# A hybrid decoder block on one core: the first pass's head outputs projected in seven products, with factor sums, gate sums and root rows moved

## The chip, the core and the metric

The kernel runs on one core of a Trainium2 chip. A core has five engines that run side by side, each with its own in-order stream of instructions: TensorE (PE), which multiplies matrices into the PSUM memory, VectorE (DVE), ScalarE (ACT), GpSimd (POOL) and SyncE (SP), which here issues the data transfers (DMAs). They meet through semaphores. The metric is the time of one execution on the device in microseconds (us), lower is better, as the median of three runs.

## The reference

A block over 2048 tokens of width D = 1024, in float32:

```
ada = silu(c) @ w_ada + b_ada;  shift, scale, gate = split(ada, 3)
h   = rms_norm(x, g_pre) * (1 + scale) + shift
pv, pg, hq, hf, hi, hg, mg_pool, mg_hgrn = split(h @ w_in)
branch_a = (pool(pv) * pool_scale * silu(pg)) @ w_pool_o     # 512 wide
o        = hgrn2(silu(hq), 1 - f, hi, log f)                 # 8 heads of 128; V is hi
branch_b = (rms_norm(o, hgrn_norm_g) * silu(hg)) @ w_hgrn_o  # 1024 x 1024
merged   = sigmoid(mg_pool) * branch_a + sigmoid(mg_hgrn) * branch_b
x + gate * rms_norm(merged @ w_out, g_post)
```

The change touches four places: V (`hi`), the gate row, `branch_b`'s projection by `w_hgrn_o`, and the preparation of `w_out`'s factors.

## The kernel before

The tokens go in two passes (p = 0 and 1) of 1024, each of two halves (t) of 512. Each float32 operand of a large product is split into a rounded part and the rest (`split`, L174: a copy on ACT, a subtraction on DVE), and a product is made of three matmuls: high by high, high by low, low by high (`three`, L352). A tile is 128 partitions by 512 columns (256 KB).

**Seven products.** A product of two 2x2 block matrices can be had from seven block products in place of eight, if sums of the blocks are multiplied. The kernel's names for the seven are B11, B21, T1, T2, T3, B22, T4. `quad` (L607) does this per head for the input projections, with T1 to T4 of h formed by `h_mix` (L594) and the weights' sums formed as they are loaded (`quad_items`, L211). `rows7` (L927) does it for a whole 1024 x 1024 projection: seven products of four row blocks by four factors by three matmuls, each of 128x512.

**The stages of a pass** are:
- V: `v_job` (L886), direct, in the first pass, in two halves of two column groups; `rows7` in the second;
- the heads, 8 of them, each with three `quad`s and the recurrence `hgrn` (L658) spread between them in steps (`tick`);
- the pool projection `a_job` (L1038), 8 jobs;
- the head outputs' projection: in the first pass `b_job` (L1048), eight jobs with two banks of 24 matmuls each, on head outputs split whole (`two_split`, L1016); in the second `b_fast` (L1096), on `rows7`. Its moving operands are sums of head outputs, formed by `g_half` (L1093) and `forms` (L1066), and split for the next product while one runs (`next_parts`, L1079);
- the output projection `y_fast` (L1138), on `rows7`, with the sums of merged columns formed by `forms("m", ...)` at the end of `b_fast`, or in `b_job`.

**Weights and their order.** `items` lists the weight tiles in the order of use. `take` (L338) hands out one and prepares some ahead (LOOK = 4) by `prep`: `plain_item` (L200) loads a tile raw and splits it, `whole_item` (L1243) does so with a prefetch two items earlier, and `again` (L195) reloads a tile that was split before and stored in DRAM, 512 KB at once. Raw tiles lie in a ring of seven (`wrp`), most other tiles in a pool of 76 (`utile`, L93).

**Factors.** The sums of weight blocks for `rows7` are formed once, ahead, by `row_factors` (L262): load four blocks, add and subtract, split some, and queue the result in `due` for storing. `htick` (L1425) does one step of it in 4 of 9 ticks of the heads. The first pass's heads form those of `w_out` ("y7") and of V ("v7", only the sums, which the second pass then splits), the second pass's heads those of `w_hgrn_o` ("b7", all seven stored split).

**The gate row.** `gate_sum` (L439) loads 8 tiles of `w_ada`, multiplies each by a column of silu(c) and adds up on DVE; `gate_out` (L453) sums over the partitions by a matmul with ones and goes through DRAM (`ggd`), from where `gg_in` (L1131) reads it before each output projection. Both halves of it lie within the first pass's `b_job`s, as do the two root rows (`r_row`, L533): matmuls that spread the inverse norms of the next pass's tokens over a tile.

**What sets the order.** The program text gives priorities. The framework that builds the kernel orders each engine's instructions by its own model of costs and buffers, so an engine's order in the trace isn't always the text's. `after` (L99) holds an instruction behind another; `gated` (L112) holds a load behind the last store. Loads and nearly all stores are on SP's queue, which is in order: a store that waits for DVE holds the loads behind it.

Of the kernel before, what the change touches and what calls it, by code (L numbers as in the profile page):

```python
# [8 lines left out]
F32 = mybir.dt.float32  # L9
# [62 lines left out]
def tile_block(ctx: ExitStack, tc: tile.TileContext, x, c, w_ada, b_ada, g_pre, g_post, w_in,  # L72
               pool_w, pool_scale, lb_logits, hgrn_norm_g, w_pool_o, w_hgrn_o, w_out,
               ident_d, mask_d, icnt_d, w_pv_t, x_t, w_quad, w_po, w_ho, out):
# [102 lines left out]
    def raw_load(name, srcs):  # L177
        raw = wrp.tile([P, T], F32, tag="wr", name=f"wr{name}")
        SP.dma_start(raw if srcs[1] is None else raw.rearrange("p (k n) -> p k n", n=srcs[1]), srcs[0])
        return raw  # L180
# [19 lines left out]
    def plain_item(key, src, n, keep_it):  # L200

        def make():
            name = f"{len(ready)}"
            if key in scr:
                return [again(key, name)]
            w = item_split(name, early.pop(key) if key in early else raw_load(name, (src, n)))
            keep(key, w, keep_it)
            return [w]
        items.append((1, make, None))
# [47 lines left out]
    def factor_step(steps):  # L257
        while due:
            store("due", *due.pop(0))
        once(steps)  # L260

    def row_factors(key, src, e, whole=(), skip=()):  # L262

        steps = []
        for i in range(4):
# [7 lines left out]
            def put(f, nm, i=i, r=r):  # L273
                if f in whole:
                    scr[key, f, i] = dram(f"scr_{key}_{f}_{i}", [P, T])
                    due.append((scr[key, f, i], r[nm]))
                    return
                w = [utile(f"rf{key}{f}{i}{z}", F32R) for z in range(2)]
                split(r[nm], w[0], w[1], e)
# [3 lines left out]

            def sums(r=r, i=i):
                r["s1"] = utile(f"rs{key}{i}")
                tt(r["s1"], r["21"], r["22"], op=ADD, e=e)

            def sub(o, a, b, r=r):
                tt(r[o], r[a], r[b], op=SUB, e=e)

            nop = lambda: None
            def both(f, g):
                return lambda: (f(), g())

            if whole:
                steps += [ld, nop, both(sums, lambda put=put: put(2, "s1")),
                          lambda sub=sub: sub("21", "11", "21"),
                          both(lambda sub=sub: sub("11", "s1", "11"), lambda put=put: (put(4, "21"), put(3, "11"))),
                          both(lambda sub=sub: sub("12", "12", "11"), lambda put=put: put(5, "12"))]
                continue  # L300
            todo = [(None, ld), (None, nop),
                    (0, lambda put=put: put(0, "11")),
                    (None, sums),
                    (1, lambda put=put: put(1, "12")),
                    (2, lambda put=put: put(2, "s1")),
                    (None, lambda sub=sub: sub("21", "11", "21")),
                    (None, lambda sub=sub: sub("11", "s1", "11")),
                    (3, lambda put=put: put(3, "11")),
                    (4, lambda put=put: put(4, "21")),
                    (None, lambda sub=sub: sub("12", "12", "11")),  # L310
                    (5, lambda put=put: put(5, "12")),
                    (6, lambda put=put: put(6, "22"))]
            steps += [g for f, g in todo if f not in skip]
# [125 lines left out]
    def gate_sum(n):  # L439
        acc = utile(f"gacc{n}")  # L440
        for kk in range(KT):
            wa = utile(f"wg{n}_{kk}")
            gated(wa, w_ada[kk * P:(kk + 1) * P, 2 * D + n * T:2 * D + (n + 1) * T])
            if kk == 0:
                V.tensor_scalar(acc, wa, cact[:, 0:1], None, op0=MUL)
            else:
                V.scalar_tensor_tensor(acc, wa, cact[:, kk:kk + 1], acc, op0=MUL, op1=ADD)
# [3 lines left out]
        return n, acc, bg, gp  # L451

    def gate_out(n, acc, bg, gp):  # L453
        ones = utile(f"ones{n}")[:, 0:P]
        G.memset(ones, 1.0)
        pg = px.tile([P, T], F32, tag="px", name=f"pgate{n}")
        PE.matmul(pg, lhsT=ones, rhs=acc, start=True, stop=True)
        V.tensor_tensor(bg, pg, bg, op=ADD)
        V.tensor_tensor(bg, gp, bg, op=MUL)
        store("gg", ggd[n], bg)  # L460
# [72 lines left out]
    def r_row(p, t, cx):  # L533

        pr = px.tile([P, T], F32, tag="px", name=f"pr{p}_{t}")
        dg = utile(f"dg{p}_{t}")
        for tk in range(NT):
# [3 lines left out]
            mm(pr[:, sl], one128, dg[:, sl], True, True)  # L541
# [452 lines left out]
    def two_out(nm, p, i, t, src, cx, stay):  # L994

        if stay and nm == "G" and p == NPASS - 1:
# [8 lines left out]
    def two_in(nm, p, i, cx):  # L1005
        for t in range(2):
            if nm == "G" and p == NPASS - 1:
# [13 lines left out]
    def sig_in(p, j, w, cx):  # L1021
# [4 lines left out]
        if nw < (1 if p == NPASS - 1 else 2):  # L1026
            cx["sm"][nj, nw] = sig_load(p, nj, nw, cx)
# [19 lines left out]

    def b_job(p, j, cx):  # L1048
        ps = [bank(f"psB{p}_{j}_{t}") for t in range(2)]
        sm = sig_in(p, j, 1, cx)  # L1050
        for half in range(2):
            w = take()
            for t in range(2):
                three(ps[t], w, [cx["gG"][4 * half + i, t] for i in range(4)], half == 0, half == 1)
        for t in range(2):
            a, b = cx["a"].pop((j, t)), sm[t]
# [515 lines left out]
```

## Time and profile before

| | us |
|---|---|
| median of 3 runs | 1751.21 |
| lowest and highest | 1750.67, 1752.98 |
| the profiled execution | 1752.19 |
| its span, first to last instruction | 1750.4 |
| ACT busy | 839.9 |
| POOL busy | 90.3 |
| TensorE's mean granted clock | 0.999 of full speed |

The stages in the profile of before: V of the first pass to about 124 us, the first pass's heads to about 685, the pool projection to 738.6, the head outputs' projection to 828.6, the output projection to 905; then the second pass. Of each slice of a fortieth of the span the page gives the busy share in tenths, and how many GB/s the DMAs moved:

```profile
DVE  4668897888988898666687265556566655676566
...
GB/s 313 266 182 312 300 279 274 285 295 267 289 300 294 277 247 279 186 203 91 231 326 182 267 252 233 249 228 214 257 240 226 230 192 206 167 252 200 250 186 265
```

The page lists groups of instructions by line, engine and operation, with the tiles that are written and read (buffer numbers left out), the count, the busy time and the mean duration of one, and the idle time of the engine ahead of them with its cause. A matmul's duration overlaps that of its neighbours, so what one costs is the distance from start to start. The chain of work follows the last instruction back to what released each step.

### The profile page before, as it was taken

The numbers are of one execution on the slowest core, as the hardware profiler recorded it, in microseconds if no ns is written. First come the engines' busy times: TensorE is split into PE (matmuls) and PEld (weight loads), VectorE is DVE, ScalarE is ACT, GpSimd is POOL, SyncE is SP. The second block draws the span as 40 slices with busy tenths as digits, with TensorE's granted clock in tenths as the row PEclk, the third lists the DMA queues.
The fourth block names the chain that finished last, engine by engine and source line by source line (L and its number), as shares of the span: only waits on it lengthen the run. The fifth ranks groups of instructions, "written<-read, shape, count | busy, mean of one in ns | idle before, by whom it ended". The sixth has DMA issues, their size and how long they took to land.

```text
span 1750.4 us, 31763 instructions
## 1 busy us (share of the span) xinstructions
PE 1725.4 (99%) x11853; PEld 1410.7 (81%) x11853; DVE 1208.6 (69%) x2516; ACT 839.9 (48%) x1953; POOL 90.3 (5%) x152
## 2 busy tenths in 40 slices
PE   7999999999999999999999999999999999999998
PEld 4788888888888887888888888888788788888886
DVE  4668897888988898666687265556566655676566
ACT  4746657566565565411655335344354352433243
POOL 1100000000010010000020000000000000000002
PEclk9999999999999999999999999999999999999999
DMA  9758877787888767562695877766776766575757
GB/s 313 266 182 312 300 279 274 285 295 267 289 300 294 277 247 279 186 203 91 231 326 182 267 252 233 249 228 214 257 240 226 230 192 206 167 252 200 250 186 265
DMA packets 193588, 428.47 MB, mean 245 GB/s; under 512 B 19565, under 2 KB 44826, under 8 KB 193434
## 3 DMA queue, kind: packets, MB, share of 16 engines
q1 hardware_dynamic: 184218, 409.66, 68.6%
q10 hardware_dynamic: 9216, 16.78, 2.5%
q8 instruction: 93, 1.52, 0.4%
q14 instruction: 61, 0.50, 0.1%
HBM read 264.36 MB, written 162.00 MB: 244 GB/s over the span
## 4 chain that ended last, share of the span: by engine, by line
PE 89%; DMA 5%; DVE 3%; ACT 1%; issue 1%; SPq 0%; POOL 0%; DVEq 0%; POOLq 0%; ACTq 0%
PE pafq L350 10%; PE pam L350 9%; PE pagp L350 9%; PE pem L350 5%; PE psB L350 5%; PE psA L350 5%; PE pefq L350 5%; PE pegp L350 5%; PE psa L350 4%; PE psV L350 3%; PE ray L350 3%; PE po L350 3%; PE pbfq L350 2%; PE pbgp L350 2%; PE pbm L350 2%; PE raB L350 2%
## 5 line engine op out<-in xcount | busy, mean ns | idle before, releaser
L175 ACT CAST whl<-wr 128x512 fp32r<-128x512 f32 x176 | 109.2, 621 | 99.6 <-PE psB L350 30.1
L175 DVE TENSOR_TENSOR whl<-wr,whl 128x512 fp32r<-128x512 f32 x176 | 120.3, 687 | 53.1 <-ACT whl L175 47.7
L350 PE MATMUL pam<-hT,whl 128*128 128x512 f32 x384 | 129.1, 397 | 0.4 <-ACT c12m L616 0.3
L350 PE MATMUL pagp<-hT,whl 128*128 128x512 f32 x384 | 128.2, 395 | 0.1
L350 PE MATMUL pafq<-hT,whl 128*128 128x512 f32 x384 | 126.2, 389 | 0.8 <-ACT c12fq L616 0.8
L714 DVE COPY_PREDICATED PT<-mask,psa 128x256 f32<-128x256 uint8 x160 | 86.4, 549 | 46.3 <-PE psa L350 46.3
L350 PEld LDWEIGHTS pagp<-hT,whl 128*128 128x128 f32 x384 | 72.1, 188 | 16.0 <-issue 0.5
L350 PEld LDWEIGHTS pafq<-hT,whl 128*128 128x128 f32 x384 | 72.1, 188 | 15.9 <-ACT c12fq L616 0.9
L350 PEld LDWEIGHTS pam<-hT,whl 128*128 128x128 f32 x384 | 72.1, 188 | 15.5 <-ACT c12m L616 0.7
L350 PE MATMUL psA<-Ph,whl 128*128 128x512 f32 x256 | 82.4, 395 | 0.1
L350 PE MATMUL psV<-whl,hB 128*128 128x512 f32 x256 | 79.6, 394 | 1.2 <-ACT hB L1324 1.1
L480 DVE TENSOR_TENSOR K<-K,TT 128x256 f32<-128x256 f32 x192 | 80.2, 424 | 0.1
L350 PE MATMUL psB<-Gh,whl 128*128 128x512 f32 x256 | 79.8, 392 | 0.0
L350 PE MATMUL pam<-lT,whl 128*128 128x512 f32 x192 | 74.9, 390 | 0.0
L350 PE MATMUL pagp<-lT,whl 128*128 128x512 f32 x192 | 74.9, 390 | 0.0
L350 PE MATMUL pafq<-lT,whl 128*128 128x512 f32 x192 | 74.7, 389 | 0.0
L175 ACT CAST whl<-wri 128x512 fp32r<-128x512 f32 x52 | 32.3, 622 | 83.1 <-PE raB L350 27.3
L350 PEld LDWEIGHTS psa<-X,K 128*32 128x32 f32 x2816 | 50.1, 110 | 26.1 <-issue 19.9
L350 PE MATMUL psa<-X,K 128*32 128x48 f32 (+2 forms) x2816 | 60.7, 208 | 0.0
L350 PEld LDWEIGHTS psV<-whl,hB 128*128 128x128 f32 x256 | 47.4, 188 | 13.9 <-ACT hB L1324 1.4
L825 POOL TENSOR_SCALAR ss<-ss 128x4 f32<-128x4 f32 x32 | 10.0, 312 | 901.5 <-ACT junk L824 901.3
L350 PEld LDWEIGHTS psA<-Ph,whl 128*128 128x128 f32 x256 | 48.0, 188 | 10.4 <-ACT Ph L175 0.5
(556 smaller groups left out, 4728.3 us busy)
## 6 DMA issues: line engine op xcount, KB each, us to landing
wr<-in_w_quad_dram SPq DMA_DIRECT2D x88, 256.0 KB, 4.0
whl<-scr_y SPq DMA_DIRECT2D x36, 512.0 KB, 4.3
sm<-Sd SPq DMA_DIRECT2D x64, 256.0 KB, 4.8
scr_b<-rfb SPq DMA_DIRECT2D x56, 256.0 KB, 3.0
whl<-scr_b SPq DMA_DIRECT2D x28, 512.0 KB, 4.1
scr_y<-rfy SPq DMA_DIRECT2D x40, 256.0 KB, 2.1
x<-in_x_dram SPq DMA_DIRECT2D x32, 256.0 KB, 4.3
wa<-in_w_ada_dram SPq DMA_DIRECT2D x32, 256.0 KB, 6.2
```

The lines of the kernel that those rows point to most:

```text
L175: return A.copy(hi, src32), (e or V).tensor_tensor(lo, src32, hi.bitcast(F32), op=SUB)
L350: return PE.matmul(o, lhsT=l, rhs=r, start=start, stop=stop, skip_group_check=True)
L480: return (e or V).tensor_tensor(o, a, b, op=op)
L714: V.copy_predicated(dst.rearrange("p (c q) a b -> p c q a b", c=NT), m, src.rearrange("p c (a b) -> p c a b", b=b).unsqueeze(2) .broadcast ...
L825: G.tensor_scalar(ss, ss, 1.0 / P, EPS, op0=MUL, op1=ADD)
```

## The change

- **Seven products in the first pass.** `b_job`, `two_split`'s use for head outputs and the host's rearranged copy of `w_hgrn_o` go; both passes use `g_half`, `forms` and `b_fast`. 
- **Factors.** Those of `w_hgrn_o` are formed in the first pass's heads, beside those of `w_out`; the second pass's heads form none. Of their seven, B11, B21 and B22 are no longer stored split: both passes load them raw and split them (`FORMED["b7"]`). The steps of `row_factors` are grouped anew, 68 in all as before.
- **V's factor sums** are formed in the first pass's V stage, from the raw tiles that were loaded there: these are kept (`vraw`; all but the first four lie in the pool of 76, and those of the second column group are loaded two items ahead), and `v_sums` adds them up at four places and queues four stores for each. The loads of V's weights in the heads go.
- **The gate** is loaded in eight steps and added in eight within `b_fast` (`gate_steps`). Its ones-matmul (`gate_sum`) and the rest (`gate_out`) lie in the first pass's output projection, which uses the tiles directly; DRAM is only for the second pass.
- **The root rows** lie in `b_fast`'s first two steps, in a bank of the ring of four.
- **Sums.** `b_fast` forms the merged columns' sums later: the first two sets at (B22, 2) and (T4, 0), the last two in the first two steps of `y_fast`. The scaling of the next pass's rows has written-out places, (T1, 1) to (T3, 0), in place of one for each step.

```diff
+    vraw = {}
+    def v_sums(i):
+        b11, b12, b21, b22 = (vraw.pop(z) for z in ((0, 2 * i), (0, 2 * i + 1), (1, 2 * i), (1, 2 * i + 1)))
+        V.tensor_tensor(b22, b21, b22, op=ADD)
+        V.tensor_tensor(b21, b11, b21, op=SUB)
+        V.tensor_tensor(b11, b22, b11, op=SUB)
+        V.tensor_tensor(b12, b12, b11, op=SUB)
+        for f, r in ((2, b22), (4, b21), (3, b11), (5, b12)):
+            scr["v7", f, i] = dram(f"scr_v7_{f}_{i}", [P, T])
+            due.append((scr["v7", f, i], r))
...
+    def gate_steps():
+        def ld(n, q):
+            gpart[n, q] = []
+            for kk in (2 * q, 2 * q + 1):
+                wa = utile(f"wg{n}_{kk}")
+                gated(wa, w_ada[kk * P:(kk + 1) * P, 2 * D + n * T:2 * D + (n + 1) * T])
+                gpart[n, q].append((kk, wa))
+        def add(n, q):
+            for kk, wa in gpart.pop((n, q)):
+                if kk == 0:
+                    gsum[n] = utile(f"gacc{n}")
+                    V.tensor_scalar(gsum[n], wa, cact[:, 0:1], None, op0=MUL)
+                else:
+                    V.scalar_tensor_tensor(gsum[n], wa, cact[:, kk:kk + 1], gsum[n], op0=MUL, op1=ADD)
...
-    FORMED = {"v7": (w_in[:, O_I:O_I + D], (0, 1, 6), (2, 3, 4, 5)), "y7": (w_out, (0, 1), ()), "b7": (w_hgrn_o, (), ())}
+    FORMED = {"v7": (w_in[:, O_I:O_I + D], (0, 1, 6), (2, 3, 4, 5)), "y7": (w_out, (0, 1), ()), "b7": (w_hgrn_o, (0, 1, 6), ())}
...
+            flush_due()
             v_job(p, t, grp, q, cx)
             if t == 0:
-                for _ in range(3 if p == 0 else 1):
+                for _ in range(3):
                     once(late)
-            elif q != 2:
+                if q > 1:
+                    v_sums(q - 2)
+            elif (grp, q) in ((0, 2), (1, 1)):
+                v_sums(2 + grp)
+            else:
                 once(mixes)
...
-        for key in (("y7", "v7"), ("b7",))[p]:
+        for key in (("b7", "y7"), ())[p]:
...
+        def b_step(nm, i):
+            if nm == "B11" and i < 2:
+                once(rows_r)
+            if nm in ("B21", "T1", "T2"):
+                once(g_loads)
+            if nm in ("T1", "T2"):
+                for _ in range(1 + i % 2):
+                    once(g_adds)
+        last_forms = b_fast(p, cx, [lambda: forms("g", 3, cx["g32"])], b_step)
```

More of the change, by code (lines that the diff above doesn't have):

```diff
@@ L273, in put @@
             def put(f, nm, i=i, r=r):
[L274 to L277, printed above, removed]
                 w = [utile(f"rf{key}{f}{i}{z}", F32R) for z in range(2)]
-                split(r[nm], w[0], w[1], e)
+                split(r[nm], w[0], w[1])
                 scr[key, f, i] = dram(f"scr_{key}_{f}_{i}", [P, 2 * T])
@@ L282, in put, with sub @@
                     due.append((scr[key, f, i][:, z * T:(z + 1) * T], w[z].bitcast(F32)))
+            def sub(o, a, b, r=r):
+                tt(r[o], r[a], r[b], op=SUB)
             def sums(r=r, i=i):
                 r["s1"] = utile(f"rs{key}{i}")
[L286 to L313, printed above, removed]
+                tt(r["s1"], r["21"], r["22"], op=ADD)
+            steps += [ld, lambda: None, sums,
+                      lambda put=put, sub=sub: (put(2, "s1"), sub("21", "11", "21")),
+                      lambda sub=sub: sub("11", "s1", "11"),
+                      lambda put=put: put(3, "11"),
+                      lambda put=put, sub=sub: (put(4, "21"), sub("12", "12", "11")),
+                      lambda put=put: put(5, "12")]
+            if 6 not in skip:
+                steps.append(lambda put=put: put(6, "22"))
         return steps
@@ L437, in tile_block, with gate_rows @@
     ggd = dram("ggd", [2, P, T])
[L439 to L447, printed above, removed]
+    gsum, gpart = {}, {}
+    def gate_steps():
[12 more added lines that the diff above has]
+                    V.scalar_tensor_tensor(gsum[n], wa, cact[:, kk:kk + 1], gsum[n], op0=MUL, op1=ADD)
+        return ([lambda z=z: ld(z // 4, z % 4) for z in range(8)], [lambda z=z: add(z // 4, z % 4) for z in range(8)])
+    def gate_rows(n):
         bg, gp = utile(f"bg{n}"), utile(f"gp{n}")
@@ L450, in gate_sum, with gate_out @@
         gated(gp, g_post[0:1, n * T:(n + 1) * T].broadcast_to([P, T]))
[L451 to L458, printed above, removed]
+        return bg, gp
+    def gate_sum(n):
+        pg = bank(f"pgate{n}")
+        g = gsum[n]
+        mm(pg, one128, g, True, True)
+        A.copy(g, pg)
+    def gate_out(n, bg, gp):
+        V.tensor_tensor(bg, gsum.pop(n), bg, op=ADD)
         V.tensor_tensor(bg, gp, bg, op=MUL)
@@ L533, in r_row @@
     def r_row(p, t, cx):
-        pr = px.tile([P, T], F32, tag="px", name=f"pr{p}_{t}")
+        pr = px.tile([P, T], F32, tag="px", name=f"pr{p}_{t}") if p == 0 else bank(f"pr{p}_{t}")
         dg = utile(f"dg{p}_{t}")
@@ L1046, in a_job @@
             tick()
[L1048 to L1056, printed above, removed]
-            tt(b, ps[t], b)
-            tt(a, a, b, op=ADD)
-            cx["m32"][t, j] = a
-            if t == 0:
-                part(p, ("B11", "B21")[j % 2] + "m", j // 2, a, cx)
-            elif j % 2 == 1:
-                forms("m", j // 2, cx["m32"])
     def forms(name, i, src):
```

122 lines of the change are left out of this document (56 added, 66 removed).

## The prediction

> **What bounds the kernel now.** I began with the page: who is busy.
>
> ```profile
> span 1750.4 us, 31763 instructions
> ...
> PE 1725.4 (99%) x11853; PEld 1410.7 (81%) x11853; DVE 1208.6 (69%) x2516; ACT 839.9 (48%) x1953; POOL 90.3 (5%) x152
> ```
>
> TensorE (PE) is busy 99% of the span (the stretches quoted further down have its granted clock at 1.00). A busy share can hide pauses, since matmuls are pipelined, so I asked next what PE waits for, over the whole span, longest first.
>
> ```profile
> PE xT L518 <- DVE x L505: 6.2, 2, 5.4
> PE pst L142 <- DMA rows<-in_hgrn_norm_g_dram: 4.6, 1, 4.6
> PE pr L350 <- DVE dg L540: 1.3, 2, 0.6
> PE po L350 <- DVE SC L812: 1.2, 1, 1.2
> ...
> PE rxV1B L350 <- DVE whl L175: 0.8, 1, 0.8
> ```
>
> The two long waits are in the first microseconds, which the change does not aim at. After them no wait reaches 1.5 us. So between the start and the tail the time is the number of matmuls times their pitch, and what other engines do costs nothing until it makes PE wait. Third, the stages that the change rebuilds, in the chain of work that ended last: columns are start and duration in us, then the tile and the count of matmuls.
>
> ```profile
> 738.80 32.64 PE psB L350 x144
> 772.30 36.31 PE psB L350 x160
> ...
> 1590.31 21.76 PE rxB1B L350 x96
> 1612.07 11.13 PE rxB1T L350 x48
> 1623.20 21.76 PE raB L350 x96
> 1644.96 6.12 PE rxB1T L350 x27
> 1651.08 5.01 PE rxB1T L350 x21
> 1656.09 10.88 PE raB L350 x48
> ```
>
> The first pass projects the head outputs as psB, directly. The second pass already does it in seven products (rxB1B, rxB1T, raB): 336 matmuls between 1590.31 and 1656.09 + 10.88 = 1666.97. 48 matmuls in a row take 10.88 us, a pitch of 0.2267 us. The direct form has more of them:
>
> ```profile
> L350 PE MATMUL psB<-Gh,whl x256: 387/389/799, 738.6 to 828.4; 128*128 128x512 f32 x128
> L350 PE MATMUL psB<-Gl,whl x128: 387/389/799, 738.9 to 828.2; 128*128 128x512 f32 x128
> ```
>
> 256 + 128 = 384. The 389 ns here is one matmul from start to end; it overlaps its neighbours, so the pitch is what one costs.
>
> **The change part by part.** The stages as stretches of the span, in order: V of the first pass, its heads (two rows), its psB stage, most of the second pass's heads, the second pass's seven products. Columns: from and to, length, the busy time (and count) of PE, weight loads, DVE, ACT and POOL, then clock, DMA share and GB/s.
>
> ```profile
> 63.60:124.00 60.40, 60.40 (x268) 49.97 (x267) 46.05 (x73) 38.42 (x67) 2.70 (x3) 1.00 0.49 159
> 140.00:600.00 460.00, 459.81 (x3750) 378.29 (x3749) 395.43 (x873) 273.40 (x666) 24.49 (x36) 1.00 0.80 287
> 600.00:685.00 85.00, 83.92 (x680) 68.49 (x682) 76.15 (x165) 48.83 (x116) 6.82 (x6) 1.00 0.71 252
> 738.80:828.80 90.00, 90.00 (x397) 73.59 (x397) 58.03 (x93) 16.45 (x27) 0.41 (x2) 1.00 0.49 158
> 1012.00:1530.00 518.00, 516.37 (x4237) 425.08 (x4236) 309.35 (x740) 220.09 (x573) 18.34 (x28) 1.00 0.68 223
> 1590.30:1667.00 76.70, 76.70 (x338) 62.95 (x337) 44.19 (x72) 19.64 (x36) 0.00 (x0) 1.00 0.68 233
> ```
>
> *Seven products in the first pass.* 7 products x 4 row blocks x 4 factors x 3 matmuls = 336 instead of 384, with the same 128x512 shape. 48 fewer, and 48 have a row of their own: -10.88 us. All of it lies on the path, because PE is the path. The gate sums' four matmuls and the 16 short ones of the two root rows (pr) are as many as before; they move, within one stage or into the next, at no cost to the total.
>
> The Trainium skill (TensorE: Matmul & The Clock Gate, Back-to-back issue gap) gives about 131 ns as the sustained spacing of matmuls with 512 columns in a real kernel; by it the 48 would be worth an estimated 6.3 us. The trace does not agree: its pitch is 0.2267 us, and it decides.
>
> *What the seven products cost other engines.* Behind the first bar stand the busy us of the group and the mean ns of one; the DMA rows give size and median us to landing.
>
> ```profile
> L175 ACT CAST whl<-wr 128x512 fp32r<-128x512 f32 x176 | 109.2, 621 | 99.6 <-PE psB L350 30.1
> L175 DVE TENSOR_TENSOR whl<-wr,whl 128x512 fp32r<-128x512 f32 x176 | 120.3, 687 | 53.1 <-ACT whl L175 47.7
> ...
> L447 DVE SCALAR_TENSOR_TENSOR gacc<-wg,small,gacc 128x512 f32<-128x512 f32 x14 | 10.4, 745 | 2.3 <-DMA wg<-in_w_ada_dram 2.2
> L540 DVE TENSOR_SCALAR dg<-ident,rst 128x128 f32<-128x128 f32 x4 | 1.0, 280 | 0.0
> ...
> scr_b<-rfb SPq DMA_DIRECT2D x56, 256.0 KB, 3.0
> whl<-scr_b SPq DMA_DIRECT2D x28, 512.0 KB, 4.1
> ```
>
> VectorE (DVE) first: in the second pass the stage takes 44.19 us of it. The first pass now needs that, plus 12 splits of factors that are loaded raw (0.687 each, 8.2), 16 gate additions (at most 0.745 each, 11.9), and eight short scalings for the root rows (0.28 each, 2.2): 66.5 of about 78 us, 85%. The stretch from 600 to 685 runs at 76.15 / 85 = 90% of DVE, and the list of waits names no wait there above 1.5 us. So I charge nothing here; without that cover each microsecond that DVE is late costs one. DMA: the old stage moved 90 us x 158 GB/s = 14.2 MB. Out go 16 loads of 256 KB (4.2 MB), in come 12 of 256 KB and 16 of 512 KB (11.5 MB): 21.5 MB in 78 us, 276 GB/s. The heads carry 287 for 460 us.
>
> *Heads of the first pass.* Out go the V factors (16 sums, 16 loads, 16 stores), in come those of this projection (16 sums, 16 loads, 16 splits, 32 stores). Net: 16 splits, 16 x 0.687 = 11 us of DVE and 16 x 0.62 of ACT, and 16 stores of 256 KB. DVE goes from 471.6 to 482.6 of 545 us, 87% to 89%. Hidden, by the same 90%.
>
> *Heads of the second pass.* They lose 16 loads, 28 splits, 16 sums and 56 stores. One of those stores had stood in PE's way:
>
> ```profile
> 1354.76 5.13 DMA scr_b<-rfb
> 1359.99 0.36 DVE SC L812
> ```
>
> DVE had to wait 5 us for a tile whose buffer a store was still reading, and PE then waited the 1.2 us quoted in the list above. That store is gone: -1.2 us. In the second pass's projection 12 factors come as raw loads and are split: +8.2 us of DVE on 44.19 in 76.7, 68%; nothing.
>
> *The V stage of the first pass.* Sixteen sums (16 x 0.687 = 11 us of DVE) and 16 stores enter, and 12 to 16 raw tiles live longer, four of them in the seven-deep ring of raw weights. DVE has 60.40 - 46.05 = 14.4 us free. What could be late next is the head stage's first mixed operand:
>
> ```profile
> 115.53 1.28 DVE L175 TENSOR_TENSOR lT<-h,hT 128x512 fp32r<-128x512 f32 x2
> ...
> 126.29 0.39 PE L350 MATMUL pefq<-hT,whl 128*128 128x512 f32 x1
> ```
>
> The last parts (lT) are done at 116.8; the product that reads them first starts at 126.3, and reaches the fourth of them 9 matmuls (2.0 us) later. That is 11.5 us of slack against at most 11 us of new DVE work, part of which falls into idle time. Hidden, but with the least margin of all parts. Bounds: 0, and the 3.0 us that a store of a factor (scr_b) takes to land, if the stores then hold up a buffer.
>
> *The output projection of the first pass* takes over 8 of the mixing sums (5.5 us) and four loads of gate rows, and drops a store and a reload of the gate rows, two of each. The scaling of the next pass's rows comes later but still three products (33 us) before it is read. No charge.
>
> *New waits, all together.* No row shows them. Bounds: below nothing, if the 0.8 us at rxV1B goes, since what is queued there moves; above, several like the 1.2 and 3.0 us rows, say 6 us. I take +1.0 us, near the 0.8 and 1.2 rows, since those are what this kernel's late DVE has cost so far.
>
> *Sum against the profiled execution:* its time is 1752.19, its span 1750.4, with 1.8 around it. 1752.19 - 10.88 - 1.2 + 1.0 = 1741.1. The median of the runs is 1751.21, 0.98 lower: **1740.1 us**, 0.63% less.
>
> **The rivals.**
>
> *A. Part of the gain is handed back.* DVE is at 85 to 90% in three stages; if the 11 us of new splits in the heads, or the V sums, are half exposed, 5.5 us return: 1745.6. For: the margins above. Against: the 600 to 685 row. 14%.
>
> *B. DVE is already what sets the heads' pace.* Then all 11 us show, and the time is 1751.1, no change. For: a chain through DVE in each head, the SC row among them. Against: the second pass's heads have DVE at 309.35 / 518 = 60% and are no quicker for it: 518 us for 4237 matmuls are 0.122 us for one, 545 us for 3750 + 680 are 0.123. 4%.
>
> *C. The matmuls do not set the stage.* The weight loads are busy only 81%; if something else paces the stage, the 48 are worth less than 10.88 us, at the worst nothing, and only the 1.2 and the 1.0 remain: 1751.0. Against: the second pass's 336 take 76.7 us where the first pass's 384 take 90. 2%. The Trainium skill (Perfetto Trace Analysis, Identifying the Most-Contended Engine) holds matmul busy time to be a bad measure of the distance to the roofline and the weight loads' share a good one. By that rule PE has headroom; the two stages' lengths speak against it here.
>
> *D. Slower.* In the new stage the gate weights arrive in eight steps of two loads, each into one of the 76 general buffers, on the same in-order queue (SP) as the factors. If no buffer is free, the queue stands until DVE or PE frees one, up to a product later (10.88 us), and the factors behind it wait too. Four factors are prepared ahead: three of 12 matmuls each, 8.2 us, less the 4.1 us of a factor's load (whl<-scr_b) leave 4.1 us of cover. One such hold costs PE 6.8 us; two undo the gain; three give 1740.1 + 20.4 = 1760.5.
>
> ```profile
> SPq L197 <- PE rxB1T L350: 16.2, 8, 4.6
> ```
>
> Against: in the second pass the same stage's factor loads are held 4.6 us at most, and PE waits for nothing. For: the gate tiles are new there. 5%.
>
> **How the numbers follow.** The forecast has 75%. It reaches from 1737.0 (1740.1 without the 1.0 of new waits, without the 0.8 at rxV1B, and 1.2 us, half the spread of the three runs from 1750.67 to 1752.98) to 1740.1 + 5 = 1745.1, new waits at their bound of 6. A overlaps it from 1743 and ends near 1748. The range of 1737 to 1747 leaves out the end of A, then B, C and D, and 2 in 100 of the forecast's own below 1737. A change of 0.2%, 3.5 us, is about what a measurement of this kernel can tell from none. Faster: forecast and nearly all of A, 0.88. Same: B and C with the end of A, 0.07. Slower: D, 0.05.
>
> **What would show it.** Right: the first pass's head projection has 336 matmuls in 76 to 79 us, DVE there near 85%; no PE wait above 1.5 us between 60 us and the end; no SC wait of PE in the second pass's heads. Wrong: PE waiting for whl behind a DMA in that stage (D); for lT at the start of the heads (the V stage); for SC, PT or whl with DVE over 90% in the first heads (A, B); or a head projection still near 90 us (C).

## The result, and the profile after

The changed kernel takes 1761.78 us (median of 6 runs, 1759.31 to 1762.7) against 1751.85 for the kernel before, run beside it (6 runs, 1750.67 to 1752.98): a ratio of 1.0053, 95% interval 1.0041 to 1.0066. It is slower by half a per cent, where 0.63% less was forecast. The profiled execution took 1759.31 us, 1.8 more than its span.

First the page, who is busy:

```profile
span 1757.5 us, 31659 instructions
...
PE 1719.3 (98%) x11805; PEld 1403.7 (80%) x11805; DVE 1223.1 (70%) x2548; ACT 854.2 (49%) x1975; POOL 91.8 (5%) x150
```

The work did go: 48 matmuls fewer (11805 for 11853), and PE is busy 6.1 us less. Yet the span is 7.1 us longer. So PE now stands, and the second question is again what it waits for, longest first:

```profile
PE rxy0T L350 <- DVE y L495: 7.8, 1, 7.8
PE xT L533 <- DVE x L520: 5.3, 1, 5.3
PE pst L142 <- DMA rows<-in_hgrn_norm_g_dram: 4.6, 1, 4.6
PE psV L350 <- ACT whl L175: 3.6, 3, 1.6
...
PE raB L350 <- DMA whl<-scr_b: 1.1, 1, 1.1
...
PE ray L350 <- DMA whl<-scr_y: 1.0, 1, 1.0
```

The start's two waits (xT, pst) are old. New are one stop of 7.8 us in the first pass's output projection (rxy0T), three in the V stage (psV for whl) and a row of waits near 1 us.

The stages, cut at the first matmul of each (V1, B1, y1: the second pass's V, head and output projections):

| us | V | heads | pool proj. | head proj. | output proj. | V1 | heads and pool | B1 | y1 |
|---|---|---|---|---|---|---|---|---|---|
| before | 123.6 | 561.7 | 53.4 | 90.0 | 78.5 | 77.3 | 605.7 | 76.7 | 83.6 |
| after | 129.8 | 561.9 | 53.2 | 80.7 | 90.6 | 77.0 | 603.5 | 76.6 | 84.3 |
| difference | +6.2 | +0.2 | -0.1 | -9.3 | +12.0 | -0.3 | -2.2 | -0.1 | +0.7 |

The gains came (head projection, second pass's heads). Two stages next to them, which the prediction had charged with nothing, cost 18.2 us.

**The head projection**, in the stretch view (as in the prediction: PE, weight loads, DVE, ACT, POOL, clock, DMA share, GB/s):

```profile
744.90:825.60 80.70, 78.94 (x353) 64.47 (x352) 61.77 (x104) 27.71 (x49) 0.00 (x0) 1.00 0.70 240
```

PE has 353 matmuls here (the 336, 16 short ones of the two root rows, and one that reaches in from a neighbouring stage); DVE is busy 61.77 / 80.7 = 77%. From start to start, less the pitch, PE stands 1.3 us for a factor (raB for whl from scr_b, 1.1 in the list of waits) and 0.8 for the root rows.

**The output projection.** The chain of work that ended last, at the stop:

```profile
828.50 1.72 PE pgate L350 x4
...
844.29 7.29 DMA h<-in_x_t_dram
...
851.61 0.69 DVE h L495
852.30 0.60 DVE lT1m L175
852.90 0.60 DVE h L495
853.50 0.60 DVE lT1m L175
854.11 0.60 DVE h L495
854.71 0.60 DVE lT2m L175
855.31 0.60 DVE h L495
855.91 0.60 DVE lT2m L175
856.51 0.61 DVE y L495
...
857.17 4.93 PE rxy0T L350 x12
```

Read it from the end. PE's product T1 needs the PSUM banks of B11 and B21, which the four y instructions empty. DVE works in order, and ahead of y stand eight scalings of the next pass's rows (h; the chain shows the last four), each behind its load of x_t; between them, the splits for T1 and T2. The program text puts these scalings behind y, at (T1, 1) to (T3, 0); that they stand ahead of it is the framework's order. The load that the chain goes through landed at 851.6. SP's own list, of after and then of before, says why so late:

```profile
833.29 0.42 SPq L115 DMA_DIRECT2D bg<-in_b_ada_dram  x1
833.77 0.43 SPq L115 DMA_DIRECT2D gp<-in_g_post_dram  x1
834.24 0.43 SPq L115 DMA_DIRECT2D bg<-in_b_ada_dram  x1
834.77 0.38 SPq L115 DMA_DIRECT2D gp<-in_g_post_dram  x1
835.26 1.51 SPq L179 DMA_DIRECT2D wri<-in_w_in_dram  x3
840.38 0.33 SPq L110 DMA_DIRECT2D ggd<-bg  x1
840.76 1.88 SPq L115 DMA_DIRECT2D h<-in_x_t_dram  x4
```

```profile
774.82 0.33 SPq L110 DMA_DIRECT2D ggd<-bg  x1
...
832.19 5.57 SPq L115 DMA_DIRECT2D h<-in_x_t_dram  x8
```

The same eight loads went out from 832.19 before, 3.6 us into the stage. Now they go out from 840.76, 15.2 us into it: the queue comes to the gate rows only at 833.29, after some 7 us for a raw weight's buffer in the ring, and then three raw weights and a store of the gate row (ggd), for which SP waits 3.5 us until DVE has made it, still stand ahead of them. Before, both these stores lay in the head projection, at 774.82 and 810.96. What the stop costs beyond itself is in the granted clock (last but two):

```profile
848.90:857.10 8.20, 0.43 (x2) 0.01 (x1) 7.25 (x13) 7.78 (x17) 0.00 (x0) 0.84 0.98 381
857.00:861.00 4.00, 3.83 (x9) 3.06 (x10) 4.00 (x8) 2.72 (x5) 0.00 (x0) 0.50 0.02 6
```

After 8.2 us without work, 4 us run at half clock: 9 matmuls, nearly all with 0.427 us from start to start for 0.227, 2 us more. The sum for this stage: stop 8.0, half clock 2.0, the gate sums' matmuls 1.7 (they stood in the head projection before), two late operands of T4 near 903 and 907 (ray) 2.3, together 14.0; 2.0 less are the waits of 1.1 us and the second root row that before had in it.

**The V stage.** SP's list again, after:

```profile
44.33 1.69 SPq L179 DMA_DIRECT2D wr<-in_w_in_dram  x3
46.43 0.33 SPq L179 DMA_DIRECT2D wue<-in_w_in_dram  x1
47.09 4.74 SPq L563 DMA_DIRECT2D h<-in_x_t_dram  x8
52.28 2.26 SPq L179 DMA_DIRECT2D wup<-in_w_in_dram  x4
```

and before:

```profile
44.58 0.33 SPq L179 DMA_DIRECT2D wre<-in_w_in_dram  x1
45.25 2.39 SPq L179 DMA_DIRECT2D wr<-in_w_in_dram  x4
47.97 4.54 SPq L548 DMA_DIRECT2D h<-in_x_t_dram  x8
```

The raw weights of the second column group (wup), in the pool of 76 now, go out at 52.28 behind eight loads of x_t. In the kernel before, four such raw weights (wr, in the ring) went out at 45.25 ahead of the x_t loads. The three at the head of the new list (wr, in the ring) are others, those of the second half, which nobody reads before 80.70; they stand ahead of the last raw weight of the first group (wue; wre before). ACT, which splits the weights, waits for both late ones:

```profile
51.47 0.62 ACT L175 CAST whl<-wue 128x512 fp32r<-128x512 f32 x1 [1.43 <-DMA wue<-in_w_in_dram]
57.54 1.28 ACT L175 CAST whl<-wup 128x512 fp32r<-128x512 f32 x2 [2.80 <-DMA wup<-in_w_in_dram]
80.70 0.61 ACT L175 CAST whl<-wr 128x512 fp32r<-128x512 f32 x1
```

SP hardly stands there: of its waits between 40 and 60 us the longest of a load for another engine's work, and so for a buffer, is 0.8 us. What is late is these loads' place in the list. PE stops at 50.8, 56.2 and 73.1 us (1.1, 1.8 and 1.2 us), with a stretch at clock 0.63 from 58.0 to 62.5. The first two stops are for these weights. The third is not: the chain there runs on DVE, through two of the V sums (67.47 to 68.79) and eight scalings of h behind them, to 74.85.

### The profile page after: what moved, and what is told of

The parts are those of the page before. It is cut to its first block, busy times and chain, and to the rows that moved or that the text cites. A ratio compares the mean times of both kernels' runs of the same rounds, so it can differ in the third digit from the quotient of the medians.

```text
span 1757.5 us, 31659 instructions
## 1 busy us (share of the span) xinstructions
PE 1719.3 (98%) x11805; PEld 1403.7 (80%) x11805; DVE 1223.1 (70%) x2548; ACT 854.2 (49%) x1975; POOL 91.8 (5%) x150
## 4 chain that ended last, share of the span: by engine, by line
PE 87%; DVE 5%; DMA 2%; ACT 1%; issue 1%; POOL 0%; SPq 0%; DVEq 0%; POOLq 0%; ACTq 0%
PE pafq L350 10%; PE pam L350 10%; PE pagp L350 9%; PE pem L350 5%; PE pefq L350 5%; PE pegp L350 5%; PE psA L350 4%; PE psa L350 4%; PE raB L350 4%; PE psV L350 3%; PE po L350 3%; PE ray L350 3%; PE pbfq L350 2%; PE pbm L350 2%; PE pbgp L350 2%; PE raV L350 2%
## 5 line engine op out<-in xcount | busy, mean ns | idle before, releaser
L350 PE MATMUL pagp<-hT,whl 128*128 128x512 f32 x384 | 128.2, 395 | 1.6 <-DVE pm L495 1.6
L175 DVE TENSOR_TENSOR whl<-wr,whl 128x512 fp32r<-128x512 f32 x152 | 103.9, 687 | 33.4 <-ACT whl L175 28.7
L175 ACT CAST whl<-wr 128x512 fp32r<-128x512 f32 x152 | 94.5, 622 | 55.1 <-issue 14.5
L175 ACT CAST whl<-wri 128x512 fp32r<-128x512 f32 x76 | 47.3, 623 | 112.5 <-PE psA L350 29.2
L175 DVE TENSOR_TENSOR whl<-wri,whl 128x512 fp32r<-128x512 f32 x76 | 51.7, 686 | 25.5 <-ACT whl L175 24.8
L677 DVE TENSOR_SCALAR F<-F 128x512 f32<-128x512 f32 x16 | 6.8, 426 | 78.3 <-ACT F L676 78.2
```

What stands on the lines that cost most here:

```text
L175: return A.copy(hi, src32), (e or V).tensor_tensor(lo, src32, hi.bitcast(F32), op=SUB)
L350: return PE.matmul(o, lhsT=l, rhs=r, start=start, stop=stop, skip_group_check=True)
L677: V.tensor_scalar(F, F, 1e-30, None, op0=MAX)
```

## The experiments

The theory: two separate losses, each of in-order queues. In the output projection DVE has the next pass's rows, late by SP's queue, ahead of y. In V the held raw tiles fill the pool, so loads come late. Rivals: DVE simply has too much to do, or the stores cost. Each ratio is against the kernel before, run beside it; where none is given, a kernel is read by its stages alone. Each kernel has one profile. V is at 129.6 to 129.8 us in the six that have its part as in the changed kernel (after, e1, e5, e6, e9, e14); but without that part, with the same instructions and nearly everywhere the same order, it is 123.0 to 124.7, and with y first the output projection takes 81.4 to 83.7. So a difference of less than 2 us between two profiles is read only with the waits that make it up. I call medians apart from 0.2% on: the kernel before has medians of 1750.43 to 1752.01 in its six series.

**e1, rows held behind y.** `after(cx["iy"])` around the scaling of the next pass's rows:

```diff
+                with after(cx["iy"]):
+                    one(k)
```

> The changed kernel with one order added: in the first pass's output projection the scaling of the next pass's rows (h times rr, 8 of them on DVE) may be issued only after the four y products that empty the first product's PSUM banks. Same loads, same DVE work. Theory Late rows (PE's 7.8 us wait there is DVE standing in order at an h tile that has not landed, ahead of the y products): the wait goes, and with it the half-clock matmuls behind it; the output projection falls from 90.6 us to 80 to 82, the whole by 9 to 10 us. Rival DVE load (8 mixing sums and 4 gate additions more than before make DVE too slow at that place): the same work has to be done, PE waits 3 us or more still, the whole falls by 4 us at most. Rival Gate row (the y products wait for bg itself): nothing changes, 0 to -1 us.

Ratio 1.0026 (1.0016 to 1.0036), output projection 86.6, the stop

```profile
PE rxy0T L350 <- DVE y L495: 2.9, 1, 2.9
```

So the rows are 5 of the 8 us, and the output projection stays above the 80 to 82 that were expected. 14 matmuls at half clock still follow (clock 0.50 from 852.6 to 858.5), though the stop is little more than a third as long.

**e2, the first two raw tiles of the second group in the ring.** `(src, None), key[2] > 1` for `(src, None), True` in `plain_item`.

> The changed kernel, but the first two raw tiles of V's second column group go to the ring of seven raw buffers in place of the pool of 76. Same sums, same stores. Theory Late raw tiles (PE's waits at 50.8 and 56.2 us come from raw tiles that were queued behind the eight x_t loads, because the pool had no free buffer): these two loads come before the x_t loads as in the kernel before; PE's wait of 1.8 us at 56.2 and the half-clock matmuls after it go; the V stage ends 3 to 5 us earlier (129.8 to 125 to 127), the whole falls by 3 to 5 us. Rival DVE load (the 16 sums delay the scaling of h and the splits): V ends within 1 us of 129.8.

V 127.7, ratio 1.0047 (1.0031 to 1.0064): 2.1 of the 6.2 us, less than I had expected. The place of these two is a part, not the whole.

**e3 and e4, thin sums, and no V part.** e3 cuts V's 16 sums to 32 of 512 columns. e4 holds nothing, sums and stores nothing, and the second pass's V takes plain blocks.

> The changed kernel with V's 16 factor sums cut from 512 columns to 32 (the other columns are left unsummed, so the second pass's V is another); loads, held tiles, stores and their waits stay. Theory Late raw tiles: the first PE waits (50.8 and 56.2 us) stay, and V ends at 127 to 130 against 129.8; DVE's 11 us are worth 3 us at most, of the later waits at 73 to 76. Rival DVE load: V ends near 123.6 to 125, as in the kernel before.

> The changed kernel without its V part: no raw tile is held, none is loaded two items ahead, no factor sums and no stores of them (the second pass takes plain weight blocks in place of the sums, so its V is another). The V stage's instructions are then those of the kernel before. Both theories: V ends at 123.6 and the whole is about 6 us shorter than the changed kernel, 1755 to 1756. If it is shorter by clearly less, V's 6.2 us lie in something that the change moved elsewhere.

V 128.1 and 124.7. With a sixteenth of the columns in the sums only 1.7 us come back; without the whole part, 5.1. e4's output projection is 92.9, its stop longer (9.5 us), though PE, DVE, ACT and SP have the same instructions in the same order up to the stop: DVE waits 3.0 us for one load of x_t there, 1.0 in the changed kernel.

**e5, gate rows loaded early; e6, that and y first.** e5 loads bg and gp in the head projection, at T3. e6 has e5 and e1, and the splits for T2 behind y as well:

```diff
+            if (nm, i) == ("T3", 0):
+                rows_g.extend(gate_rows(n) for n in range(2))
...
+            if not fin and nm == "B21":
+                if i == 2:
+                    with after(cx["iy"]):
+                        for z in range(3):
+                            next_parts(p, nm, z, "m", cx["m32"], cx)
```

> The changed kernel, with only the four loads of gate rows (bg, gp) moved forward into the head projection (at T3 of its seven products); the scaling of the next pass's rows stays ahead of y. Theory (a transfer chain: gate rows late, then the gate store that waits for them, then behind it on SP the x loads, then the scaling on DVE, then y): the x loads are issued about 4 us sooner, so PE's stop at T1 of the output projection falls from 7.8 us to 3 to 5 us, the output projection from 90.6 to 86 to 88 us, the kernel by 3 to 4 us, to about 1757. Rival (it is not the transfers but how many instructions DVE has ahead of y): the stop stays above 6.5 us and the time within 1.5 us of the changed kernel's.

> The changed kernel with three edits, all in the first pass's output projection: the scaling of the next pass's rows and the splits for T2 are held behind the four y products on DVE, and the gate rows are loaded in the head projection. Theory (everything that stands ahead of y on DVE and need not): no stop of PE at T1 above 1 us, so no matmuls at half clock after it; the output projection takes 80 to 82 us instead of 90.6 (78.5 before, and four matmuls of the gate sums more), the kernel about 9 to 10 us less than the changed one, near 1752, the same as before. Rival (the matter is that DVE as a whole has too much to do between 825 and 858 us): the wait only moves, to T2 or T3 whose operands now come later, and the stage stays above 85 us.

e5: 1761.4, ratio 1.0059 (1.0045 to 1.0073): nothing gained. Its stop at T1 is 4.6 us, as expected, and the output projection 88.7. But the head projection takes 85.1 for 80.7. SP's queue in e5, in that stage:

```profile
797.83 0.42 SPq L115 DMA_DIRECT2D bg<-in_b_ada_dram  x1
798.30 0.64 SPq L115 DMA_DIRECT2D gp<-in_g_post_dram  x1
799.04 1.01 SPq L115 DMA_DIRECT2D bg<-in_b_ada_dram  x1
800.61 0.33 SPq L115 DMA_DIRECT2D gp<-in_g_post_dram  x1
801.32 5.04 SPq L197 DMA_DIRECT2D whl<-scr_b  x4
```

Four gate loads stand ahead of four factors. PE waits for factors twice:

```profile
PE raB L350 <- DMA whl<-scr_b: 1.9, 1, 1.9
PE rxB0T L350 <- DMA whl<-scr_b: 1.7, 1, 1.7
```

Only the second is theirs: it is at 805.6, for the factor that went out at 801.32. The first is at 782.8, before these loads go out, and has half clock behind it; it is the stop that the changed kernel has at 783, behind the gate's weights (wg), which takes about 1 to 2 us in the runs. The stop behind the gate rows is rival D of the prediction in its in-order queue, though not in its full pool: SP waits at most 1.2 us for anything at these four. e6, with the same four loads, has it too (1.8 us in its list, with 7 matmuls at half clock behind it). e6: 1755.05, 1.0025 (1.0016 to 1.0035), head projection 84.3, output projection 81.7, the stop 0.6.

**e9, y first alone** (e6 without the early gate rows).

> As e6, but the gate rows are loaded where the changed kernel loads them, at the start of the output projection: only the scaling and the T2 splits are held behind y. Theory (in e6 the four loads of gate rows stood on SP ahead of the factors of the head projection and cost it 3.5 us; the rows themselves were not what y waited for): head projection back at 80.7 us, output projection 81.5 to 83, the kernel 8 to 9 us below the changed one, about 1752. Rival (the late gate rows hold y once the scaling is out of the way): output projection 84 or more, PE waiting for y 2 us or more.

1752.84, ratio 1.0011 (1.0002 to 1.002): not to be told from before. Head projection 81.3, output projection 81.7. The theory of the output projection stands: nearly 9 of the 12 us were the order of DVE's instructions ahead of y, with unchanged work. A DVE that has too much to do, the rival, would have kept them.

**e7 and e8, V's sums from the second half; e8 with e6.** `hold` for t == 1 in place of t == 0, and the four sums at the last four steps of V.

> The changed kernel, with the V factor sums taken from the second half's raw tiles instead of the first's: the same 16 sums and 16 stores, but the raw tiles are held from about 75 us on, when the first pass's x rows and the weights of the modulation have left the pool, and all four groups of sums stand in the last quarter of the V stage. Theory (the 6.2 us of the V stage are loads that stood behind x_t loads on SP because the pool of 76 had no free buffer at 45 to 52 us): V takes 124 to 126 us instead of 129.8 (123.6 before), and there is no half clock at 58 to 62 us; the kernel gains 4 to 6 us, if nothing in the output projection moves. Rival 1 (11 us more of DVE work in V are what costs): V stays at 128 or above, with PE waiting for DVE at its end or for lT at the start of the heads. Rival 2 (the 16 stores on SP): V 126 to 128, waits for whl behind stores at the start of the heads.

> The three edits of the output projection (scaling and T2 splits behind y, gate rows loaded earlier) and the V sums from the second half together. Theory (the two losses are separate, and the head projection's 9.3 us and the second pass's 2.2 us are real): V 124 to 126, head projection 80 to 81, output projection 80 to 82, the rest as in the changed kernel: 1761.8 - 5 - 9.5 = 1747, 0.2 to 0.4% faster than before. Rival (each loss returns in the next stage when it is taken away in one, since DVE or SP is what sets the pace of the first pass): 1752 or above.

e7: V 129.6, 1760.57, 1.0056 (1.0042 to 1.0069). The waits between 50 and 75 us are gone, and PE stops 2.5 us at 114.2 and runs at half clock after it. SP's queue there:

```profile
108.60 1.52 SPq L110 DMA_DIRECT2D scr_v<-wup  x2
111.00 2.13 SPq L110 DMA_DIRECT2D scr_v<-wu  x2
113.22 1.82 SPq L179 DMA_DIRECT2D wup<-in_w_in_dram  x4
```

The last four raw tiles wait behind the stores of sums. The place changed and the price did not; my 124 to 126 was wrong. e8 is at 1755.11, 1.0023 (1.0014 to 1.0032), with V 128.2 and heads 563.3: not the 1747 forecast.

**e10, half of the sums from each half of V** (on e9); **e11, its gate loads on GpSimd's queue; e12, the x_t loads of V there too.**

```diff
-                    plain_item(("v", grp, k), krow(w_in, k, O_I + grp * T), t == 0)
+                    plain_item(("v", grp, k), krow(w_in, k, O_I + grp * T), (t == 0) == (k < 4))
...
+    def side_q(dst, src):
+        with after(last["st"]):
+            return G.dma_start(dst, src)
...
-                gated(wa, w_ada[kk * P:(kk + 1) * P, 2 * D + n * T:2 * D + (n + 1) * T])
+                side_q(wa, w_ada[kk * P:(kk + 1) * P, 2 * D + n * T:2 * D + (n + 1) * T])
...
-                        xt_load(0, 1, k, cx, SP.dma_start)
+                        xt_load(0, 1, k, cx, G.dma_start)
```

> e9 with the V factor sums halved over V's two halves: blocks 0 to 3 of the contraction held from the first half's raw tiles, 4 to 7 from the second half's, and the first two raw tiles of the second column group in the ring. At no time are more than 8 raw tiles held. Theory (what costs is the number of raw tiles held in a full pool, with the loads queued behind): V 125 to 127 us (129.7 in e9 and the changed kernel, 123.6 before), the kernel 3 to 4 us below e9, about 1748.5. Rival (11 us of DVE and 16 stores cost what they cost, wherever they stand, as e7 looked): V 128 or more, with waits in the last quarter.

> e10 with the 16 loads of gate weights and the 4 of gate rows issued from GpSimd's queue instead of SP's. Theory (the stop of 1.3 us at 783 us, PE waiting for a factor from DRAM, comes from gate loads ahead of it on SP): that stop goes, the head projection takes 79 to 79.7 us, and the time is 1 to 1.5 us less than e10's. Rival (the factor is late since the DMA engines are shared or since its own buffer is late, so another queue doesn't help): head projection 80.5 or more; or loads from GpSimd's queue cost more, and it is slower than e10.

> e11 with the eight loads of x_t in V issued from GpSimd's queue too, so that the raw weights behind them on SP needn't wait until the pool has buffers for x_t. Theory (the order on SP is what makes V's weights late): V loses what is left of its waits between 50 and 80 us, 0.5 to 2 us less than e11. Rival (the pool's buffers are what is late, whichever queue asks): V within 0.5 us of e11's, since the held raw tiles themselves need pool buffers.

e10: V 126.3, but the heads take 565.3 (562.8 in e9; two waits of about 1 us near 153 and 159 us are new), so the pool projection starts at 691.6 where it starts at 692.5 in e9; 1753.55, 1.0011 (1.0002 to 1.002). e11: 1753.14, 1.0009 (1.0 to 1.0018); its head projection is 80.7 for 81.4 and PE's stop near 783 us falls from 2.0 to 1.0 us. That is the rival's figure (80.5 or more), not the 79 to 79.7 of the theory, and the medians don't tell the two kernels apart. e12: 1759.56, 1.0048 (1.0034 to 1.0062). Its V is the longest of the four, 130.1, and all of it is already lost at 41 us: the matmuls of the modulation (psa) run some 4.5 us later than in e11. The x_t loads no longer wait their turn on SP; I take it that they share the start's transfers, but no run parts that.

**e13 to e15, the V part taken apart** (all on e9; the second pass's V takes plain blocks in all three). e13 holds the raw tiles, with two one-column instructions for each four sums and no stores; e14 holds and sums, with no stores; e15 has none of it.

> e9 with the V part's raw tiles loaded and held as in the changed kernel, but only two one-column instructions in place of each four sums (so that the tiles are held as long), and no stores; the second pass's V then takes plain blocks of the weights. Against e9, V and first heads together 692.5 us from the start, and with e15 (no V part at all), this tells what the holding costs. Theory (a raw tile that is held takes a pool buffer, and the loads behind it on SP come late): V 127.5 to 129, most of the 5 us that the V part costs. Rival (DVE's 11 us of sums and the stores are what costs): V below 126.

> e9 with the V part's raw tiles and its 16 sums in full, but no stores of them; the second pass's V takes plain blocks of the weights. Theory (holding): no more than 1.5 us above e13, V 128.5 to 129.7. Rival (the 16 stores, each of which has to be read out before its buffer is free, and which stand on SP ahead of loads): V 126 or less, near e15.

> e9 without the V part: no raw tiles held, no sums, no stores; the second pass's V takes plain blocks of the weights. It leaves V's factor sums out. V 124.7 as in e4, heads 562, head projection 81, output projection 82: 5 us below e9, 1747 to 1748.5, which is what the rest of the change is worth with the output projection mended. Rival (what V gains is handed back in the heads, as in e8 and e10): start of the pool projection still at 691 to 692 us from the start, the time within 2 us of e9.

| | V | first heads end at |
|---|---|---|
| e9, all of it | 129.7 | 692.5 |
| e14, no stores | 129.7 | 691.5 |
| e13, held only | 132.5 | 694.4 |
| e15, none | 123.5 | 685.8 |
| before | 123.6 | 685.3 |

The stores cost nothing by themselves: e14 is e9 in V. e13 came out above both, and by a wait that neither has:

```profile
PE psV L345 <- ACT hB L175: 7.5, 1, 7.5
```

The planned order is another one there: SP issues seven raw weights in a row at 44.40, where the changed kernel issues three. ACT reads the first of these seven at 83.40. The last weight of the first group (wue) goes out behind them, at 49.29, and on DVE a one-column instruction on it, which waits 8.3 us, stands ahead of the modulation's last steps, for which h and then hB wait. So e13 doesn't size the holding, but shows again the price of order. The other runs size it by subtraction: of the 6.2 us between e15 and e9, the stores are nothing (e14), DVE's sums some 1.7 (e3), and the 4.5 that remain come with the held tiles and the order of loads that goes with them; of these e2 got 2.1 by two places in the ring. That a full pool is what makes the framework order them so isn't shown. e15 takes 1746.25 us, a ratio of 0.9975 (0.9965 to 0.9985): with y first and the V sums left out, the rest of the change is faster than before by 0.25%.

**e16 to e18, V's sums in the second pass's V.** On e15's base, that stage loads its 16 blocks raw, keeps them, and forms the sums between the splits. In e16 two of each four blocks are exchanged in the sums, so it computes another V; loads, sums and splits are as many. e17 has them right, loads two blocks of each four together, forms a sum of each four a product later, and moves eight scalings from T1 to T3; e18 adds e11's queue.

```diff
+        def f2(i):
+            tt(r["s1", i], r["21", i], r["22", i], op=ADD)
+            w = sp_("s1", i)
+            tt(r["21", i], r["11", i], r["21", i], op=SUB)
+            return w
```

> e9 without the V part, and the V factor sums formed where they are used: the second pass's V loads its 16 blocks once, raw, keeps them in the pool, and forms its 16 sums between the splits (12 loads and 16 stores fewer in all, nothing left out). DVE there has 50.3 us of work in 77; with 11 us more it is at 80%. Theory (the V part costs 5 us where the pool and SP are full and nothing where they are not): V 124.7, second V stage 77 to 78, the kernel 4 to 5 us below e9, 1747.5 to 1749, 0.15 to 0.25% below before. Rival (the sums hold up PE in any stage): second V stage 80 us or more, no gain on e9.

> e16 with the second pass's V factors spread: one sum of each four is formed a product later (for T2), and the eight final scalings of the first pass's output rows, which stood in T1 of that stage, come at T3. The whole of the reference is computed, with 12 loads and 16 stores fewer than in e9. In e16 the second V stage took 84.4 us against 77.0, with stops of 2.9, 1.1 and 1.1 us around T1, where 12 sums, 4 splits of sums and the scalings met on DVE. Theory (the sums cost only where DVE has no time for them): second V stage 78 to 80 us, V 123 to 124, the rest as in e15: 1747.5 to 1749.5, 0.1 to 0.2% below before. Rival (the loads of 512 KB for T1's sums, or what DVE has to do at B11, are what is late): second V stage 82 or more, 1751 or more.

> e17 with the loads of gate weights and gate rows issued from GpSimd's queue, as in e11. e11's head projection was 0.8 us shorter than e10's and its output projection 0.8 us, by one profile each, at medians 0.4 apart. Theory: 0.5 to 1.5 us below e17, 1747 to 1748.5. Rival: within 0.5 us of e17.

e16: V 123.0, second V stage 84.4; 1753.95, 1.0018 (1.0009 to 1.0027). e17: 84.5, and 3.7 us more in the second heads; 1756.23, 1.003 (1.0018 to 1.0041). e18: 1755.22, 1.0035 (1.0022 to 1.0048), not to be told from e17; its head projection takes 84.3 us, with two stops of 1.7 us, so the queue of e11 is no sure gain. DVE's share of the stage, 65% as a mean, had misled me; e17 by stretches (DVE is the third busy time):

```profile
904.00:925.00 21.00, 19.39 (x83) 15.09 (x82) 20.24 (x34) 8.35 (x15) 2.97 (x4) 1.00 0.82 293
925.00:935.00 10.00, 7.12 (x23) 5.18 (x23) 10.00 (x18) 4.74 (x9) 0.00 (x0) 0.83 0.46 171
935.00:950.00 15.00, 14.49 (x64) 11.67 (x63) 13.58 (x24) 9.60 (x17) 0.00 (x0) 1.00 0.00 1
950.00:990.00 40.00, 40.00 (x178) 33.13 (x177) 16.09 (x25) 14.02 (x25) 0.00 (x0) 1.00 0.39 131
```

DVE is all but full until 950 and at 40% after it, while the sums are all wanted for T1 to T3, the third to fifth of the seven products. No version that computes the whole reference beat the kernel before.

## Why the prediction was wrong, step by step

- **Seven products, -10.88: right in kind, and cashed.** The stage lost 9.3 us by the profile. Beside the 10.9, 1.7 went with the gate sums' matmuls into the next stage; against that, waits grew by 2.3 (1.3 for a factor, 0.8 for the root rows, the rest small), and one of the root rows came in (1.0). The stage has the forecast's matmuls at the pitch of 0.227.
- **"So I charge nothing here" for DVE in that stage: right.** 77% busy, against the 85% worked out, and no stop there that is DVE's beyond the 0.8 for dg.
- **Second pass's heads, -1.2: right, mis-sized.** Measured -2.2. The SC wait is gone; no wait of PE is listed between 1000 and 1590 us.
- **First pass's heads, "Hidden": right.** +0.2, though one wait of 1.6 us for DVE is new among them (pagp for pm, at 331 us).
- **The V stage, "Hidden, but with the least margin", bounds 0 and 3.0: failed.** It cost 6.2. The part had named that 12 to 16 raw tiles live longer, and then priced only DVE's 11 us, at the stage's end, where nothing is lost. The loss lies between 50 and 76 us: weights that come late from SP's list, then scalings of h behind V sums on DVE. e3 puts DVE's sums at some 1.7, e14 the stores at nothing; the other 4.5, by subtraction, come with the tiles held. A tile that lives longer should have been followed to the loads that are then ordered anew on SP, and to what stands behind them.
- **The output projection, "No charge": the step that failed most, 12.0 us** (1.7 of it the gate sums' matmuls, which only moved). I had asked when the scaled rows are read (three products later) and not what is queued behind them. DVE is in order: a thing that nobody needs yet stood ahead of y, which empties the banks that PE needs. The four loads of gate rows were counted, but not as places on SP's queue, and the stores of the gate row were read the wrong way: the stage doesn't drop them, it takes them over from the head projection, and the first of them holds SP for 3.5 us ahead of x_t. e1, e6 and e9 give back 4, 8.8 and 8.8 us of it by order alone.
- **"New waits, all together", +1.0, at most 6: failed in size.** The bound was several waits like those that the old trace showed. But a kernel without long waits shows none to bound by. The two stages came to 18.2, of which 1.7 is work that moved and somewhat under 4 is half clock.
- **The rivals.** The time came out near D's 1760.5, and that is luck. In-order queues are half of D's mechanism; the other half, a queue that stands since no buffer of the pool is free, isn't seen in either of the two stages that lost (in the output projection SP stands some 7 us, but for the ring of seven), and neither stage is D's. Where D placed it, PE waits 1.3 us behind the gate's weights, and 1.7 to 1.8 us more when e5 and e6 put four more loads there: a quarter of the 6.8 us that D had for one hold. Of A a small part happened, the 1.7 us of V sums. B and C did not: the heads kept their length, and the matmuls set the stage.

What stays open: why the V sums cost some 4 to 8 us in each arrangement tried (first half, that with the ring for two, second half, half and half, the second V stage). What PE waits for is seen in each (late weights, SP's stores, DVE), but a common cause is not shown. Part of the sums in each stage with room was not tried, nor the sums in the first pass's heads, their old place, beside the other factors.

## What to carry to other kernels

In a kernel that is bound by one engine, price each moved step by its place on every in-order queue: ask what now stands behind it, and whether the bound engine needs that sooner. Before a tile is kept longer for later use, find the loads that are ordered anew by it and what queues behind them. The program text's order is no answer to that; the trace's is. A mean busy share of a stage says nothing on the product in which the work falls due; cut the stage by product first.

## What the runs showed of the hardware

A stop of PE costs more than its length. All eight stops above 3 us after the start, in all the profiles (3.1 to 9.7 us), were followed by 5 to 14 recorded matmuls at 0.427 us in place of 0.227: 1 to 3 us more, whatever the length of the stop. In the clock that the traces record, every stretch of half clock after 30 us and before the end lasts 3.4, 6.8 or 10.2 us, part of which can pass in the stop itself (854.48 to 861.31 in the changed kernel, whose stop ends at 857.17; 851.72 to 858.55 in e1, whose stop ends at 852.69). Of those between 1.7 and 3 us some were and some weren't (1.95 us at 803 in e6: 7 matmuls; 2.9 us at 927 in e16: none); below 1.6 us none was, unless another stop soon followed. The Trainium skill (TensorE: Matmul & The Clock Gate, Why this matters for your kernels) warns of idle gaps above about 3 us between bursts of matmuls. The eight agree with it; stops of 1.7 to 2.5 us that led to half clock (e18 at 781, V at 56.2, e7 at 114.2) are shorter than its figure.
